# Start of the high weight blocks in 512-column tiles, and the order of products in the k-outer routine

## The chip, the core and the metric

The kernel runs on one core of one Trainium2 chip. The metric is the device time of one execution in microseconds. Before the change it is 2354.62 us, the median of 3 runs (2353.46 to 2354.73).

## The reference

Two layers of an encoder over 16 meta tokens and 256 tokens (272 rows, width 2048). Each layer projects the stream once (`w_in`, 6176 columns), runs gated linear attention on one part and 2-D neighbourhood attention on another, projects both back (`w_out`), adds and normalises, and does a squared-ReLU MLP of width 8192 with a second add and normalisation. All in float32; the meta rows are dropped at the end.

```python
def _layer(h, ...):
    proj = jnp.einsum('bld,dp->blp', h, w_in)
    ...
    y_gla = _gla_mixer(gq, gk, gv, gr, glr, gla_w_up, gla_b_up, gla_norm_w)
    y_na = _na_mixer(nq, nk, nv, na_rel_bias).astype(h.dtype)
    mix = jnp.einsum('blm,md->bld', jnp.concatenate([y_gla, y_na], axis=-1), w_out)
    h = _layer_norm(DEEPNORM_ALPHA * h + mix, ln1_w, ln1_b)
    ff = jnp.einsum('blf,fd->bld', jnp.square(jax.nn.relu(jnp.einsum('bld,df->blf', h, w_ff1))), w_ff2)
    return _layer_norm(DEEPNORM_ALPHA * h + ff, ln2_w, ln2_b)
```

Nearly all of the arithmetic is the four weight products `w_in`, `w_out`, `w_ff1` and `w_ff2`.

## The kernel before

**High and low parts.** Activations are held transposed, features on the 128 partitions and tokens along a row. Each float32 operand of a weight product is split in two fp32r parts: the high part is the value cast to fp32r (ScalarE), the low part is the value less the high part (VectorE). A product of a weight block w and an activation chunk x is the sum of three matmuls: high w by high x, high w by low x, low w by high x.

**Tiles of weights.** The host lays the weights out in tiles of 128 x 1024 words (512 KB): eight blocks of 128 x 128. `order` lists them in the order of use, `made` (line 180) takes one: a DMA from SP into `raw`, then in `halves` (line 208) a cast by ScalarE into `wh` (line 211) and a subtraction by VectorE into `wl` (line 212). `weights` keeps two tiles ahead, and each of `raw`, `wh` and `wl` has three buffers.

**Where blocks stand in a tile.** `blocks` (line 194) takes the start of the first block, the step from an even block to the odd one behind it, and the step from pair to pair, in words; `block` (line 199) gives the block j that a matmul loads, and `pairs` the same blocks for the engines that write them. A high tile is dense: first 0, step 128, pair 256 words, so that every high block starts at a multiple of 256 bytes. A low tile is 1280 words wide (`WIDE`) with gaps after `LOWS` (line 42), which has two entries, picked by the tile's flag `once`:

- `once` False: starts at 0 and 576 bytes, and every 1280 bytes from there. Modulo 256 the low blocks start at 0, 64, 0, 64, ...
- `once` True: first at 32 bytes, then every 640. Modulo 256 they start at 32, 160, 32, 160, ...

**Two kinds of tiles.** `once` is set for products over exactly the 256 tokens, almost all in layer 2, where the meta rows aren't needed any more. There the high and the low half of an activation are streamed by one matmul of 512 columns ("512-column tiles"), and the low weights by a second one of 256 columns. `TURNS` (line 43) alternates them, h w h w, sixteen matmuls a tile. The other tiles have three matmuls for each block, mostly of 272 columns (272 + 2 or 256 + 2 where a norm is folded in), in the order h l h l w w, twenty-four a tile: h is high by high, l high weights by low activations, w low weights by high activations.

**Two routines.** `by_m` (line 276) goes output by output: for each output m it takes tiles of eight k chunks (`eight`, line 232, matmuls at line 246), accumulating in one PSUM bank. `by_k` (line 257, matmuls at line 272) is used where activations become ready one after the other: it holds four outputs (eight in the form `wide`) in as many banks and goes through k two chunks at a time; a tile has the blocks of two chunks j and four outputs m, block 4j + m. It is called six times: at the start of layer 1 (`wide`, 16 tiles, while x is still being loaded and split), at the start of layer 2, after the attention of each layer (`w_out`), and in the MLP of each layer: the latter five take 8 tiles each. In layer 2's `w_out` and MLP it has 256 columns, else 272.

The order of the 24 products of a `by_k` tile is set by the sort key of line 270. Commonly it takes all 16 products with high weights, then the 8 with low weights (within each, k chunk by k chunk, the four outputs in turn). In the last tile of a routine, and in the first unless it is `wide`, `by_output` puts the output m first: for each output four products with high weights, then two with low. The very first tile of `wide` has an order of its own, since its blocks arrive in parts (`head`, line 214).

TensorE takes its instructions in program order. SP issues the DMAs of the weights in the order of `order`.

Of the kernel before, what the change touches and what calls it, by code (L numbers as in the profile page):

```python
# [8 lines left out]
F32R = mybir.dt.float32r  # L9
# [5 lines left out]
P = 128  # L15
# [11 lines left out]
WB = 1024  # L27
# [11 lines left out]
PAD = 40  # L39
PITCH = 288  # L40
WIDE = 1280
LOWS = {True: (8, P + 32, 2 * P + 64), False: (0, P + 16, 2 * P + 64)}
TURNS = {True: "hwhwhwhwhwhwhwhw", False: "hlhlwwhlhlwwhlhlwwhlhlww"}

# [12 lines left out]
class Trunk:  # L57
# [122 lines left out]
    def made(self, ap, ends, once):  # L180
        if ap is None:
            return None
        nc = self.nc
        raw = self.wp.tile([P, WB], F32, name="raw", tag="raw")
        wh, wl = self.wp.tile([P, WB], F32R, name="wh", tag="wh"), self.wp.tile([P, WIDE], F32R, name="wl", tag="wl")
        wh, wl = self.blocks(wh, 0, P, 2 * P), self.blocks(wl, *LOWS[once])
        for c in map(slice, (0,) + ends, ends):
            nc.sync.dma_start(raw[:, c], ap[:, c])
            self.halves(raw[:, c], wh, wl, slice(c.start // P, c.stop // P))
        if not ends:  # L190
            self.head(ap, raw, wh, wl)
        return wh, wl
# [64 lines left out]
    def by_k(self, acts, n, before, wide=False):  # L257

        ps = [self.pm.tile([P, 512], F32, name="mm", tag="mm") for _ in range(4)]
        if wide:  # L260
            ps += [self.bank() for _ in range(4)]
        nk = len(acts)
        for k in range(0, nk, 2):
            before(k)
            for g in range(0, len(ps), 4):
                wh, wl = self.weights()
                parts = ((wh, 0), (wh, 1), (wl, 0))
                order = [(j, p, m) for j in range(2) for p in range(3) for m in range(4)]
                by_output = k == nk - 2 or k == 0 and not wide
                order.sort(key=lambda o: (o[0], o[2] // 2) if wide and not k + g else (by_output and o[2], o[1] // 2))  # L270
                for j, p, m in order:
                    self.nc.tensor.matmul(ps[g + m][:, :n], lhsT=self.block(parts[p][0], 4 * j + m), rhs=acts[k + j][parts[p][1]][:, :n],  # L272
                                          start=k + j + p == 0, stop=k == nk - 2 and j + p == 3)
        return [p[:, :n] for p in ps]

# [836 lines left out]
def layout(inputs):  # L1112
    import numpy as np

    a = {k: np.asarray(v) for k, v in inputs.items()}
    f = np.float32
    x = np.concatenate([a["x"][0], a["meta"]], axis=0)
    o = {"xT": x.reshape(L, DC, P).transpose(2, 1, 0)}
    w = a["w_in"]
    q, k, v, r = w[:, :, 0:512], w[:, :, 512:1024], w[:, :, 1024:2048], w[:, :, 2048:3072]  # L1120
    lr, nq, nk, nv = w[:, :, 3072:3104], w[:, :, 3104:4128], w[:, :, 4128:5152], w[:, :, 5152:6176]
    c = lambda m, j: m[:, :, j * P:j * P + P]
    cols = [k, v[:, :, :512], q, v[:, :, 512:], r] + [c(m, j) for j in range(8) for m in (nq, nk, nv)]

    def tiles(m, kinds, halves=1):

        d, kk, n = m.shape
        nk = kk // P // halves
        m = m.reshape(d, halves, nk, P, n // 512, 512).transpose(0, 1, 4, 2, 3, 5)
        out = np.empty((d, halves, n // 512, nk // 2, P, WB), f)  # L1130
        for g in range(n // 512):
            s = m[:, :, g]
            for l in range(d):
                if (l, g) in kinds:
                    t = s[l].reshape(halves, nk // 2, 2, P, 512).transpose(0, 1, 3, 2, 4)
                else:
                    t = s[l].reshape(halves, nk // 8, 8, P, 4, P).transpose(0, 4, 1, 3, 2, 5)
                out[l, :, g] = t.reshape(halves, nk // 2, P, WB)
        return out if halves > 1 else out[:, 0]

    o["win"] = tiles(np.concatenate(cols, axis=2), ((0, 0), (0, 1), (1, 1)))
    w, q = o["win"][0, 0, 0], WB // 4
    o["head"] = np.stack([np.concatenate([w[:, c * q:c * q + q], o["xT"][:, c]], axis=1) for c in range(2)], axis=1)
    o["wlr"] = lr.reshape(DEPTH, DC, P, 32).transpose(0, 2, 1, 3).reshape(DEPTH, P, 512)
    o["wout"] = tiles(a["w_out"], ((0, 0), (1, 0)))
    o["wff1"] = tiles(a["w_ff1"], ((0, 2), (1, 2)))
    o["wff2"] = tiles(a["w_ff2"], (), 2)
    wup = np.zeros((DEPTH, LRK, 2, GH * GDK), f)
    for s in range(0, 96, 32):
        wup[:, s:s + 16, 0], wup[:, s + 16:s + 32, 1] = a["gla_w_up"][:, 0], a["gla_w_up"][:, 1]  # L1150
    wup[:, 96] = wup[:, 97] = a["gla_b_up"]
    o["wup"] = wup
    low = np.zeros(LRK, bool)
    low[64:96] = low[97] = True
    o["sel"] = np.stack([low, 1 - 2 * low], axis=1).astype(f)
    per = lambda m: m.reshape(DEPTH, DC, P).transpose(0, 2, 1)
    o["vec"] = np.concatenate([per(a["ln1_w"]), per(a["ln1_b"]), per(a["ln2_w"]), per(a["ln2_b"]),
                               a["gla_norm_w"].reshape(DEPTH, 2, P).transpose(0, 2, 1)], axis=2)
    o["norm"] = np.stack([a["ln2_w"][-1], a["ln2_b"][-1]])
    p = np.arange(P)  # L1160
    rb = a["na_rel_bias"]
    nab = np.zeros((DEPTH, NAH, 2, P, NKEY), f)
    qr, qc = p // 32, p % 32
    for t in range(2):
        kr = np.concatenate([p // 32, np.arange(32) // 8])
        kc = np.concatenate([t * 32 + p % 32, (32, 24)[t] + np.arange(32) % 8])
        cc = t * 32 + qc
        cs = np.clip(cc - WIN_W // 2, 0, GW - WIN_W)
        inside = (kc[None] >= cs[:, None]) & (kc[None] < cs[:, None] + WIN_W)
        dr = kr[None] - qr[:, None] + WIN_H - 1  # L1170
        dc = np.clip(kc[None] - cc[:, None], -(WIN_W - 1), WIN_W - 1) + WIN_W - 1
        nab[:, :, t, :, :160] = np.where(inside, rb[:, :, dr, dc], f(NEG))
    o["nab"] = nab.reshape(DEPTH, 8, 4, P, NKEY).transpose(0, 1, 3, 2, 4)
    xor = p[:, None] % 32 ^ p[None, :32]
    lev = np.where(xor == 0, 0, np.floor(np.log2(np.maximum(xor, 1))) + 1)
    o["mask"] = np.stack([lev == i + 1 for i in range(5)], axis=1).astype(f)
    o["ident"] = np.eye(P, dtype=f)
    qm = np.zeros((NM, NK2), f)
    qm[:, :32] = NEG
    o["qmask"] = qm  # L1180
    return {k: np.ascontiguousarray(v) for k, v in o.items()}
# [24 lines left out]
```

## Time and profile before

| what | value |
|---|---|
| median of 3 runs | 2354.62 us |
| the profiled execution's own time | 2354.79 us |
| its span, from first to last instruction | 2353.0 us |
| granted TensorE clock, mean | 0.999 |
| matmuls | 18180 |
| weight tiles loaded (512 KB each) | 766, beside the parts of the first two |
| HBM read | 414.03 MB |

The page's first part gives the busy time of each engine: PE is the matmuls of TensorE, PEld its weight loads, DVE is VectorE, ACT ScalarE. [...] The fourth part follows the work that ended last back to the start. In the timeline a row is a group of equal instructions in sequence: start in us, time to the end of the last, engine, line, operation, what it writes and reads, shape, count, and in brackets how long the engine had been idle and what ended it. In a window's row stand the time and the busy time and count of PE and PEld, the granted clock, and the DMA's share and rate.

### The profile page before, as it was taken

Reading aid. Unit: us, or ns where it says so; the run is one execution under the profiler, and the core shown is the slowest. Engines: PE = TensorE matmul, PEld = TensorE weight load, DVE = VectorE, ACT = ScalarE, POOL = GpSimd, SP = SyncE. Lnnn points to the kernel's source line nnn. Section 1 sums busy time; section 2 is a strip of 40 time slices with the busy share of each in tenths; the row PEclk is TensorE's granted clock in tenths of the full one; section 3 lists DMA queues with packets and bytes.
Section 4 is the critical chain, followed back from the end, with each engine's and each line's share of the span. In section 5 each row is a group of like instructions: output and inputs, shape, how many; then the busy total and the mean of one; then the engine's idle time right before and its main releaser. Section 6 shows DMA issues by size and latency. Waiting matters only on the chain.

```text
span 2353.0 us, 44603 instructions
## 1 busy us (share of the span) xinstructions
PE 2342.2 (100%) x18180; PEld 2222.5 (94%) x18180; DVE 1528.2 (65%) x2432; ACT 1213.0 (52%) x2100; POOL 130.2 (6%) x200
## 2 busy tenths in 40 slices
PE   9999999999999999999999999999999999999998
PEld 9999999999999999999999899999988888888888
DVE  5588777775544455557576887778766555666655
ACT  5666664564433344444456666655644333444443
POOL 0021110100000000000020121101000000000000
PEclk9999999999999999999999999999999999999999
DMA  8454445555555555555555454555566656566564
GB/s 256 153 164 155 152 141 179 170 178 181 180 180 179 180 180 180 181 180 178 179 190 165 154 173 154 162 170 186 184 191 190 187 188 187 188 189 213 191 190 147
DMA packets 118301, 419.02 MB, mean 178 GB/s; under 512 B 13512, under 2 KB 14024, under 8 KB 118096
## 3 DMA queue, kind: packets, MB, share of 16 engines
q1 hardware_dynamic: 117808, 415.65, 55.9%
q8 instruction: 142, 2.33, 0.4%
q10 hardware_dynamic: 288, 0.52, 0.1%
q14 instruction: 63, 0.52, 0.1%
HBM read 414.03 MB, written 2.10 MB: 177 GB/s over the span
## 4 chain that ended last, share of the span: by engine, by line
PE 96%; DVE 1%; ACT 1%; DMA 1%; issue 0%; SPq 0%; DVEq 0%; ACTq 0%
PE mm L246 86%; PE mm L272 5%; PE bg L783 1%; DMA raw<-in_win 1%; PE mm L722 1%; PE bg L583 1%; DVE wl L212 0%; PE bg L272 0%; ACT wh L211 0%; PE bg L429 0%; DMA xraw<-in_xT 0%; PE mm L748 0%; DVE acc L1011 0%; PE bg L634 0%; PE bg L909 0%
## 5 line engine op out<-in xcount | busy, mean ns | idle before, releaser
L212 DVE TENSOR_TENSOR wl<-raw,wh 128x1024 fp32r<-128x1024 f32 (+1 forms) x770 | 941.8, 1224 | 657.1 <-ACT wh L211 648.7
L211 ACT CAST wh<-raw 128x1024 fp32r<-128x1024 f32 (+1 forms) x770 | 805.1, 1046 | 905.9 <-PE mm L246 669.8
L246 PE MATMUL mm<-x,wh 128*128 128x272 f32 (+3 forms) x5376 | 1099.3, 309 | 0.1
L246 PEld LDWEIGHTS mm<-x,wh 128*128 128x128 f32 x5376 | 803.6, 188 | 51.6 <-PE mm L722 0.6
L246 PE MATMUL mm<-x,wl 128*128 128x272 f32 (+3 forms) x3264 | 753.4, 283 | 0.3 <-DVE wl L212 0.2
L246 PEld LDWEIGHTS mm<-x,wl 128*128 128x128 f32 x3264 | 548.3, 188 | 0.6 <-DVE wl L212 0.6
L246 PE MATMUL mm<-y,wh 128*128 128x272 f32 (+2 forms) x2128 | 477.3, 320 | 0.0
L246 PEld LDWEIGHTS mm<-y,wh 128*128 128x128 f32 x2128 | 328.9, 188 | 29.9
L246 PE MATMUL mm<-u,wh 128*128 128x272 f32 (+2 forms) x1552 | 347.0, 320 | 0.0
L246 PE MATMUL mm<-y,wl 128*128 128x272 f32 (+1 forms) x1408 | 338.8, 282 | 0.0
L246 PEld LDWEIGHTS mm<-u,wh 128*128 128x128 f32 x1552 | 239.4, 188 | 21.5
L246 PE MATMUL mm<-u,wl 128*128 128x272 f32 (+1 forms) x1024 | 246.1, 282 | 0.0
L246 PEld LDWEIGHTS mm<-y,wl 128*128 128x128 f32 x1408 | 242.2, 188 | 0.0
L246 PEld LDWEIGHTS mm<-u,wl 128*128 128x128 f32 x1024 | 176.2, 188 | 0.0
L272 PE MATMUL mm<-x,wh 128*128 128x272 f32 (+1 forms) x512 | 73.4, 288 | 1.0 <-DVE x L295 0.5
L272 PEld LDWEIGHTS mm<-x,wh 128*128 128x128 f32 x512 | 67.5, 189 | 1.5 <-DVE x L295 0.7
L999 POOL TENSOR_SCALAR acc<-acc,vec 128x272 f32<-128x272 f32 (+1 forms) x24 | 41.9, 1751 | 273.6 <-DVE acc L1011 155.0
L560 ACT COPY U<-S 128x272 f32<-128x272 f32 (+1 forms) x104 | 40.4, 429 | 20.6 <-DVE S L569 19.7
L871 DVE TENSOR_TENSOR acc<-acc,mm 128x256 f32<-128x256 f32 (+1 forms) x71 | 30.2, 425 | 31.3 <-PE mm L246 30.7
L569 DVE TENSOR_TENSOR S<-S,dec 128x272 f32<-128x272 f32 (+1 forms) x112 | 46.6, 445 | 3.7 <-ACT U L560 2.7
L294 ACT CAST u<-ft 128x272 fp32r<-128x272 f32 (+1 forms) x64 | 26.3, 410 | 41.8 <-DVE ft L827 41.7
L571 POOL TENSOR_TENSOR dec<-dec 128x272 f32<-128x272 f32 (+6 forms) x56 | 30.2, 539 | 239.8 <-DVE S L569 239.8
(265 smaller groups left out, 1631.5 us busy)
## 6 DMA issues: line engine op xcount, KB each, us to landing
raw<-in_wff SPq DMA_DIRECT2D x512, 512.0 KB, 3.7
raw<-in_win SPq DMA_DIRECT2D x190, 512.0 KB, 3.9
raw<-in_wout SPq DMA_DIRECT2D x64, 512.0 KB, 3.6
nb<-in_nab SPq DMA_DIRECT2D x16, 352.0 KB, 4.1
xraw<-in_xT SPq DMA_DIRECT2D x7, 272.0 KB, 5.9
out<-out SPq DMA_DIRECT2D x5, 256.0 KB, 3.1
brow<-in_norm SPq DMA_DIRECT2D x4, 256.0 KB
gw<-in_wup SPq DMA_DIRECT2D x4, 196.0 KB
```

Of the source, the lines that this page charges most:

```text
L211: self.nc.scalar.copy(h, r)
L212: self.wl = self.nc.vector.tensor_tensor(lo, r, h.bitcast(F32), ALU.subtract).ins
L246: mm(o, lhsT=self.block(w, j), rhs=rhs, start=first and not i, stop=last and i == len(TURNS[once]) - 1)
L272: self.nc.tensor.matmul(ps[g + m][:, :n], lhsT=self.block(parts[p][0], 4 * j + m), rhs=acts[k + j][parts[p][1]][:, :n], start=k + j + p == ...
L294: self.nc.scalar.copy(hi, src)
L560: nc.scalar.copy(U[:, lv % 4, j, :w].rearrange("p (n t h) -> p n t h", t=2, h=hb), bass.AP(S.tensor, S.offset + 2 * j * L, [S.ap[0], [2 * ...
L569: tt(o, o, totals(lv, odd, w), ALU.mult)
L571: nc.gpsimd.tensor_tensor(d[1], d[1], d[0], ALU.mult)
L583: nc.tensor.matmul(ps[b * 32:b * 32 + 32, o:o + w], lhsT=k[:, c:c + 32], rhs=q[:, r:r + w], start=True, stop=True)
L722: nc.tensor.matmul(ps[hh][:, t * NKEY:t * NKEY + NKEY], lhsT=q[hs, NM + t * P:NM + t * P + P], rhs=k[hs, t, :], start=True, stop=True)
L871: tt(a, a, part, ALU.add)
L999: nc.gpsimd.tensor_scalar(a, a, gain, bias, ALU.mult, ALU.add)
```

## The change

The high tile gets the width of the low one, 1280 words, and its first block a start picked by `once` (`HIGHS`): 24 words (96 bytes) in 512-column tiles, 0 as before in the others. Step and pair stay 128 and 256 words, so in 512-column tiles every high block starts 96 bytes past a multiple of 256.

In `by_k` every tile is now taken output by output, save those of the first two k chunks in the form `wide`. So that its low blocks stand as in `by_m`, block 2m + j is now that of output m and chunk j, except in those first tiles, and `layout` on the host stores the tiles so (the first tile of each of the two `wide` groups is put back into the old order).

```diff
+HIGHS = {True: 24, False: 0}
...
-        wh, wl = self.wp.tile([P, WB], F32R, name="wh", tag="wh"), self.wp.tile([P, WIDE], F32R, name="wl", tag="wl")
-        wh, wl = self.blocks(wh, 0, P, 2 * P), self.blocks(wl, *LOWS[once])
+        wh, wl = (self.wp.tile([P, WIDE], F32R, name=nm, tag=nm) for nm in ("wh", "wl"))
+        wh, wl = self.blocks(wh, HIGHS[once], P, 2 * P), self.blocks(wl, *LOWS[once])
...
-                by_output = k == nk - 2 or k == 0 and not wide
-                order.sort(key=lambda o: (o[0], o[2] // 2) if wide and not k + g else (by_output and o[2], o[1] // 2))
+                first = wide and not k
+                order.sort(key=lambda o: (o[0], o[2] // 2) if first and not g else (not first and o[2], o[1] // 2))
                 for j, p, m in order:
-                    self.nc.tensor.matmul(ps[g + m][:, :n], lhsT=self.block(parts[p][0], 4 * j + m), rhs=acts[k + j][parts[p][1]][:, :n],
+                    self.nc.tensor.matmul(ps[g + m][:, :n], lhsT=self.block(parts[p][0], 4 * j + m if first else 2 * m + j), rhs=acts[k + j][parts[p][1]][:, :n],
...
-                    t = s[l].reshape(halves, nk // 2, 2, P, 512).transpose(0, 1, 3, 2, 4)
+                    t = s[l].reshape(halves, nk // 2, 2, P, 4, P).transpose(0, 1, 3, 4, 2, 5)
...
     w, q = o["win"][0, 0, 0], WB // 4
+    for t in o["win"][0, :2, 0]:
+        t[:] = t.reshape(P, 4, 2, P).transpose(0, 2, 1, 3).reshape(P, WB)
```

## The prediction

> **What bounds the kernel now.** I read the page first: busy time, granted clock and chain.
>
> ```profile
> PE 2342.2 (100%) x18180; PEld 2222.5 (94%) x18180; DVE 1528.2 (65%) x2432; ACT 1213.0 (52%) x2100; POOL 130.2 (6%) x200
> PEclk9999999999999999999999999999999999999999
> PE 96%; DVE 1%; ACT 1%; DMA 1%; issue 0%; SPq 0%; DVEq 0%; ACTq 0%
> L246 PE MATMUL mm<-x,wh 128*128 128x272 f32 (+3 forms) x5376 | 1099.3, 309 | 0.1
> ACT wh L211 <- PE mm L272: 38.0, 20, 2.7
> ```
>
> TensorE fills the span, the clock is never held back, 96% of the chain that ended last is TensorE, and the largest group waited 0.1 us in all. The last row, from the list of waits, is the reverse direction: ScalarE waits for TensorE to release a high buffer. So time can only come from the pace of the products (the step from one matmul's start to the next one's), and be lost where the new order makes TensorE wait. A matmul's own duration (309 ns) is longer than its step and tells nothing about pace; I take steps from starts.
>
> The second view is a window wholly inside the 512-column tiles, with the groups by shape that count them; then the timeline of TensorE at five places.
>
> ```profile
> 1700.00:1800.00 100.00, 100.00 (x573) 87.58 (x573) 1.00 0.61 188
> L246 PE MATMUL mm<-x,wh 128*128 128x512 f32 x1152 | 405.3, 395 | 0.0
> L246 PE MATMUL mm<-y,wh 128*128 128x512 f32 x688 | 242.3, 394 | 0.0
> L246 PE MATMUL mm<-u,wh 128*128 128x512 f32 x496 | 175.0, 394 | 0.0
> ```
>
> 573 products in 100 us are 175 ns each, or 350 ns for a pair of one 512-column high and one 256-column low product. There are 1152 + 688 + 496 = 2336 such pairs: some 817 us, a third of the span.
>
> ```profile
> 1240.11 2.19 PE L272 MATMUL mm<-x,wh 128*128 128x272 f32 x16
> 1242.13 1.16 PE L272 MATMUL mm<-x,wl 128*128 128x272 f32 x8
> 1243.13 0.67 PE L272 MATMUL mm<-x,wh 128*128 128x272 f32 x4
> ...
> 1246.13 0.40 PE L246 MATMUL mm<-x,wh 128*128 128x512 f32 x1
> ```
>
> This is the k-outer routine at 272 columns. A tile in the old order (16 high products, then 8 low) takes 1243.13 - 1240.11 = 3.02 us; the last tile, which is already taken output by output, 3.00. The same 24 products in the m-outer routine:
>
> ```profile
> 433.16 0.65 PE L246 MATMUL mm<-y,wh 128*128 128x272 f32 x4
> ...
> 433.90 0.65 PE L246 MATMUL mm<-y,wh 128*128 128x272 f32 x4
> ...
> 434.63 0.41 PE L246 MATMUL mm<-y,wh 128*128 128x272 f32 x2
> ```
>
> Twelve products take 1.47 us, so a tile takes 2.94. At 256 columns (k-outer; then the one slim group of the m-outer routine):
>
> ```profile
> 1546.43 2.08 PE L272 MATMUL mm<-y,wh 128*128 128x256 f32 x16
> 1548.35 1.11 PE L272 MATMUL mm<-y,wl 128*128 128x256 f32 x8
> 1549.30 0.28 PE L272 MATMUL mm<-y,wh 128*128 128x256 f32 x1
> ...
> 2328.50 0.63 PE L246 MATMUL mm<-y,wh 128*128 128x256 f32 x4
> ...
> 2331.34 0.28 PE L246 MATMUL mm<-y,wh 128*128 128x256 f32 x1
> ```
>
> In the first tile the sixteen highs, all of whose blocks start at a multiple of 256 bytes, step by (1548.35 - 1546.43) / 16 = 120.0 ns; the eight lows, whose blocks start alternately 0 and 64 bytes past one, by 0.95 / 8 = 118.75. Shape, clock and activations are the same; what differs is where the weights start. The slim group, whose low starts are mixed as well, takes 2.84 us for its 24 products against 2.87: again 1.25 ns each. So the start of a weight block seems to be worth about a nanosecond of pace, in a kernel that is nothing but pace. That is the lever of this change.
>
> **The change, part by part.** The built programs hold the same instructions on every engine: products, casts, subtractions and DMAs. POOL keeps its order, SP swaps two pairs of issues, ScalarE moves 36 instructions and VectorE 93 by a few places, none of them around the wait priced below. The high tile grows from 1024 to 1280 words, and what is allocated behind it moves by whole multiples of 256 bytes. These cost nothing: ScalarE and VectorE are at 52% and 65%, and TensorE, the cover, is busy all the time; should a cast come late, 1 us of it would be 1 us of the span.
>
> *k-outer order.* Six middle tiles of each routine go from 3.02 to 2.94 us, its first and last from 3.00 to 2.94, since order and low starts (0, then 64, for the two k) become those of the m-outer routine: 6 x 0.08 + 2 x 0.06 = 0.60 us. Three routines run 272 columns without the wide form: -1.8. Two run 256 columns, 2.865 to 2.84 over 8 tiles each: -0.4. The wide one has 14 changed tiles (the first pair keeps its order), some -1.0.
>
> Against it, each tile now needs its low weights after 4 products, not 16, some 1.5 us sooner, and the second activation after 2 instead of 8. Behind the waiting product everything on TensorE queues. Where are lows late? In the layer-2 routine:
>
> ```profile
> 1225.02 2.17 PE L272 MATMUL mm<-x,wh 128*128 128x272 f32 x16
> 1225.07 1.43 DVE L212 TENSOR_TENSOR wl<-raw,wh 128x1024 fp32r<-128x1024 f32 x1
> 1227.03 1.17 PE L272 MATMUL mm<-x,wl 128*128 128x272 f32 x8
> ```
>
> VectorE ends these lows at 1226.50. Sixteen highs covered that (first low at 1227.03); four cover until 1225.02 + 0.49 = 1225.51. TensorE then stands for 1.0 us: +1.0. Next tile's lows (VectorE again, 1.2 us on) are then in time. In the wide routine:
>
> ```profile
> 32.15 1.22 DVE L212 TENSOR_TENSOR wl<-raw,wh 128x1024 fp32r<-128x1024 f32 x1 [2.65 <-ACT wh L211]
> 32.53 2.19 PE L272 MATMUL bg<-x,wh 128*128 128x272 f32 x16
> ...
> 36.37 0.79 DVE L295 TENSOR_TENSOR x<-xraw,x 128x272 fp32r<-128x272 f32 x2
> ...
> 36.87 0.39 PE L272 MATMUL mm<-x,wh 128*128 128x272 f32 x1 [0.53 <-DVE x L295]
> ...
> 39.48 2.19 PE L272 MATMUL bg<-x,wh 128*128 128x272 f32 x16
> ```
>
> By the tile of 32.53 TensorE would be some 0.4 us early, but the lows end at 33.37, so its last 20 products end at 33.4 + 2.45 = 35.9 instead of 35.6. The next tile needs the second low activation (36.37 + 0.79 = 37.16) in its fourth product: 37.2 + 21 x 0.1225 = 39.8 instead of 39.48. Five more tiles at 0.06 to 0.08 win the 0.3 back: 0 net. The later release of the high buffer (after product 22 instead of 16) falls on the 38.0 us that ScalarE waits anyway, with casts two tiles ahead. k-outer in sum: -1.8 - 0.4 + 1.0 + 0 = -1.2 us; bounds -3.2 (no wait is new) and +0.8 (the waits stay, the pace gains only at half).
>
> *High blocks 96 bytes on.* In a 512-column tile the low blocks start alternately 32 and 160 past a multiple of 256, and the highs move from 0 to 96: each load then starts 64 bytes (modulo 256) from the load before it, the spacing of the 118.75 ns lows. No row shows this spacing at 512 columns, so it is bounded: gain at most the 3.3 ns per product between 3.02 and 2.94 over 24 (4672 products: -15.4 us); loss at most what an extra piece costs, from the 274-column group:
>
> ```profile
> 1218.91 0.67 PE L246 MATMUL mm<-x,wh 128*128 128x274 f32 x4
> ...
> 1219.67 0.67 PE L246 MATMUL mm<-x,wh 128*128 128x274 f32 x4
> ...
> 1220.43 0.67 PE L246 MATMUL mm<-x,wh 128*128 128x274 f32 x4
> ```
>
> Six products take 0.76 us, 126.7 ns each against 122.5 at 272. Two more columns at 272's rate (122.5 / 272) are 0.9, so 3.3 ns is something else, such as one more piece to fetch; on 2336 high loads, +7.7. Between -15.4 and +7.7 I take the row it is nearest to, the 1.25 ns of the two 256-column readings (equal activations, only starts differ), on both products of a pair, since the distance to the load before changes for both: 4672 x 1.25 ns = -5.8 us.
>
> [...]
>
> *Sum.* The profiled execution took 2354.79 us (span 2353.0 and 1.8 around it): 2354.8 - 1.2 - 5.8 = 2347.8. The median of the runs, 2354.62, is 0.2 lower: 2347.6.
>
> **Rivals** (the -1.2 stays in each unless said).
> A, the forecast: 1.25 ns on both products, 2347.6.
> B, more of it: the spacing brings the whole 3.3 ns to both products, 2354.6 - 1.2 - 15.4 = 2338.0. For it: 512-column tiles have the most weights at one start. Against: their lows are shifted already.
> C, half of it: only the 256-column product gains, since in the 512-column one a load has twice the time: 2336 x 1.25 = 2.9, 2350.5. For it: the long product's share of the 350 ns is about twice a load's step of 118.75, so a load beside it has slack.
> D, starts don't matter, and the highs' part does nothing: 2353.4. For it: the readings of 1.25 ns are at the edge of what 10 ns of timeline resolve. Against: two of them agree.
> E, slower: a 512-byte block 96 past a boundary spans one more piece than one at 0, each high load gets 3.3 ns longer, and as the low product beside it is no longer than a load, TensorE waits for it: 2354.6 - 1.2 + 7.7 = 2361.1. It decides from 0.5 ns per pair on, where it eats the -1.2. For it: the 274-column step. Against: the lows, shifted by 32 and 160, don't show it in a pair of 350. [...]
> F, new waits in the k-outer routines (second activations, reordered VectorE work) cost 3 us more than counted and highs gain little: 2356.4.
>
> **How the numbers follow.** Chances: A 0.40, B 0.16, C 0.09, D 0.13, E 0.18, F 0.04. A measurement of this kernel tells about 0.2%, 4.7 us, from no change. Faster by more than that are A and B, 0.56; C, D and half of F lie within, 0.24; E and half of F are slower, 0.20. The range 2338 to 2360 leaves out half of B and somewhat over half of E, under 0.2. A's own range, 0.6 to 2 ns per product, is 2344 to 2351.
>
> **What would show it.** A window in the 512-column tiles with more than 573 products in 100 us (577 for A, 584 for B, 573 for D, 568 for E). k-outer tiles of 2.94 us instead of 3.02, and a wait of about 1.0 us for VectorE's lows at 1225.5. The wide routine ending at the same time. I am wrong if pairs keep at 350 ns, or if line 272 shows several new waits.

## The result, and the profile after

The changed kernel takes 2341.65 us (median of 6 runs, 2340.3 to 2343.35) where the kernel before takes 2353.78 (6 runs, 2353.46 to 2354.73, the three of the time before among them). The ratio is 0.9948, with a 95% interval of 0.9935 to 0.996: 12.1 us faster. The forecast was 2347.6, with 2338 to 2360 as its range: 7.0 us below the time before of 2354.62. The direction was right; the gain is 12.1 us where 7.0 were forecast.

The page of the changed kernel, its lines for the busy engines, the granted clock, the chain that ended last, and the largest group:

```profile
PE 2328.5 (99%) x18180; PEld 2215.7 (95%) x18180; DVE 1527.6 (65%) x2432; ACT 1212.0 (52%) x2100; POOL 130.9 (6%) x200
PEclk9999999999999999999999999999999999999999
PE 96%; DVE 2%; ACT 1%; DMA 1%; issue 0%; SPq 0%; DVEq 0%; ACTq 0%
L247 PE MATMUL mm<-x,wh 128*128 128x272 f32 (+3 forms) x5376 | 1094.5, 309 | 0.1
```

The picture is the old one: as many matmuls, the clock never held back (0.999 both times), TensorE 96% of the chain. No cover has gone and no bottleneck has moved; the same products pass sooner. The profiled execution took 2342.16 us against 2354.79, span 2340.4 against 2353.0.

The same window of the 512-column tiles as in the prediction, products of `by_m` alone:

```profile
1700.00:1800.00 100.00, 100.00 (x585) 88.52 (x584) 1.00 0.63 190
```

It holds 585 products where it held 573. The forecast wanted 577, rival B 584. The timeline of TensorE inside these tiles (only the highs of four pairs are shown):

```profile
1999.93 0.39 PE L247 MATMUL mm<-x,wh 128*128 128x512 f32 x1
...
2000.27 0.39 PE L247 MATMUL mm<-x,wh 128*128 128x512 f32 x1
...
2000.62 0.39 PE L247 MATMUL mm<-x,wh 128*128 128x512 f32 x1
...
2000.96 0.39 PE L247 MATMUL mm<-x,wh 128*128 128x512 f32 x1
```

Three pairs take 1.03 us, 343 ns each where they took 350. To see in which product that lies, I took from the trace every step (one matmul's start to the next one's) in uninterrupted stretches of 512-column tiles whose activations lie without a gap (some 2010 pairs), and their means. An "even" high block is followed by a low block at the first of the two low starts, an "odd" one by the second. In ns:

```
                 512-column step     256-column step     pair
                 even      odd       even      odd       even     odd
before           231.4     233.4     117.3     117.9     348.7    351.3
after            226.8     226.8     115.1     118.3     341.9    345.1
```

The long product gained 5.6 ns (232.4 to 226.8), the short one 0.9 (117.6 to 116.7), a pair 6.5 in its mean (350.0 to 343.5): 2010 pairs make 13.1 us.

Where in the execution does the gain come? I followed the start of the same product in both profiles. The difference, this run less before, in us:

```
at (us, about)                      after    highs only   order only
end of the wide by_k          54    +0.25      -0.79        -0.82
start of by_k, layer 2      1221    -0.79      -0.65        -1.96
its end                     1246    -0.90      -0.66        -2.27
start of by_k, w_out        1527    -0.30      -0.23        -2.21
its end                     1552    -0.38      -0.23        -2.29
end of w_out's m-outer      1620    -0.41      -1.40        -1.45
start of by_k, MLP          1667    -0.40      -1.39        -1.44
its end                     1690    -0.50      -1.39        -1.55
end of 512-column tiles     2328   -12.55     -13.44        -1.55
```

(The two other columns are the first two experiments below. Executions differ by one or two us in the wide routine, those of one and the same kernel too (50.21 and 52.23 us, below), so only differences down a column count, from that routine's end on.) After 1690 us each column with the highs at 96 gains 12.05 us in one stretch, and the one with the highs at 0 gains nothing: (2328 - 1690) / 0.350 = 1823 pairs at 6.5 ns are 11.8. Ahead of that the changed kernel stands only 0.5 us better than the old one. So the 12 us are the pace of the 512-column tiles, and the new order of `by_k` is worth little by itself.

That has its parts. The k-outer tiles did become faster. The timeline of TensorE, first and last row of one tile of layer 2's routine, and then of one at 256 columns:

```profile
1239.16 0.65 PE L273 MATMUL mm<-x,wh 128*128 128x272 f32 x4
...
1242.10 0.53 PE L273 MATMUL mm<-x,wh 128*128 128x272 f32 x3
...
1546.08 0.64 PE L273 MATMUL mm<-y,wh 128*128 128x256 f32 x4
...
1548.93 0.64 PE L273 MATMUL mm<-y,wh 128*128 128x256 f32 x4
```

1242.10 - 1239.16 = 2.94 us at 272 columns (before 3.02), 2.85 at 256 (before 2.87). Taken from the start of a routine's first product to that of the first product behind it, the two routines of layer 1 went from 26.52 to 25.94 us and from 24.10 to 23.51, and to just these times in every kernel with the new order below. These are the 0.6 us each of the forecast, and they make up the step from +0.25 to -0.79 in the table. In layer 2 `w_out` and the MLP won 0.1 us each.

But TensorE waits in new places. Its list of waits (waiting product and line, releaser; us in total, times, longest), after:

```profile
PE mm L273 <- DVE x L296: 1.4, 2, 0.9
...
PE mm L247 <- DVE wl L213: 0.9, 2, 0.7
PE mm L273 <- DVE wl L213: 0.6, 1, 0.6
```

and before:

```profile
PE mm L272 <- DVE wl L212: 0.6, 1, 0.6
PE mm L272 <- DVE x L295: 0.5, 1, 0.5
...
PE mm L246 <- DVE wl L212: 0.2, 1, 0.2
```

The first row is the wide routine. The second product of a tile now needs the low part of the first activation, where in the old order the fifth did. Its timeline (VectorE makes the low parts of both activations in the row ahead):

```profile
17.20 0.79 DVE L296 TENSOR_TENSOR x<-xraw,x 128x272 fp32r<-128x272 f32 x2
...
17.69 0.75 PE L273 MATMUL mm<-x,wh 128*128 128x272 f32 x3 [0.47 <-DVE x L296]
...
36.55 0.79 DVE L296 TENSOR_TENSOR x<-xraw,x 128x272 fp32r<-128x272 f32 x2
...
37.05 0.74 PE L273 MATMUL mm<-x,wh 128*128 128x272 f32 x3 [0.91 <-DVE x L296]
```

Waits of 0.47 and 0.91 us, where before there was one of 0.53. Reckoned as in the column above, this execution stands at -0.37 at 10 us and at +0.25 at the routine's end, 0.6 us lost. The product that waits the second time starts at 37.05, when the first of the two low parts is done (36.99); by the trace the fourth, which needs the second low part, comes 0.36 us behind it. So it is the first low part that TensorE stands for, not the second as the prediction had it. But 0.6 us is no price of the new order. The routine takes 50.21 us here and 52.23 in another execution of the same kernel (the last experiment), 47.9 to 50.6 in the nine other kernels with the new order, and 48.6 to 49.95 in the three with the old one. In this stretch ScalarE waits for the DMAs of the weights and of x, five times by 1.5 to 3.7 us before and four times by 2.4 to 3.1 us after (waits over 1.5 us), here for example:

```profile
34.33 1.05 ACT L212 CAST wh<-raw 128x1024 fp32r<-128x1024 f32 x1 [3.11 <-DMA raw<-in_win]
```

These waits differ from one execution to the next, and what the new order is worth in the wide routine is not shown.

The wait for the lows of line 247 is a place that the prediction did not look at, the norm of layer 2, in 512-column tiles and outside `by_k`. After (timeline; VectorE's lows, the accumulation just ahead of them, and the product that waits):

```profile
1558.88 1.23 DVE L213 TENSOR_TENSOR wl<-raw,wh 128x1024 fp32r<-128x1024 f32 x1 [1.51 <-ACT wh L212]
...
1565.76 0.42 DVE L938 TENSOR_TENSOR s<-s,sqv 128x256 f32<-128x256 f32 x1
...
1566.10 1.22 DVE L213 TENSOR_TENSOR wl<-raw,wh 128x1024 fp32r<-128x1024 f32 x1
...
1567.37 0.39 PE L247 MATMUL mm<-y,wl 128*128 128x256 f32 x1 [0.66 <-DVE wl L213]
```

and VectorE's lows in the same stretch before:

```profile
1561.34 1.22 DVE L212 TENSOR_TENSOR wl<-raw,wh 128x1024 fp32r<-128x1024 f32 x1
...
1564.32 1.22 DVE L212 TENSOR_TENSOR wl<-raw,wh 128x1024 fp32r<-128x1024 f32 x1
```

Before, VectorE took a tile's lows about every 3 us. After, its program has the norm's accumulations between two of them, 7.2 us apart (1558.88 to 1566.10), and TensorE runs dry. From 1552 to 1620 us the pace should bring some 1.2 us, and highs alone do (-0.23 to -1.40); the changed kernel gets 0.03, so about 1.1 us are lost, and order alone loses 0.84 at the same place.

One more small loss: from 1246 to 1527 us some 300 pairs stream activations whose two halves lie apart (the second starts 128 bytes past a multiple of 256). These take 354 ns in the mean after and 352 before: +0.6 us in the column.

### The profile page after: what moved, and what is told of

It is laid out like the page before. It is cut to its first block, busy times and chain, and to the rows that moved or that the text cites. A ratio compares the mean times of both kernels' runs of the same rounds, so it can differ in the third digit from the quotient of the medians.

```text
span 2340.4 us, 44604 instructions
## 1 busy us (share of the span) xinstructions
PE 2328.5 (99%) x18180; PEld 2215.7 (95%) x18180; DVE 1527.6 (65%) x2432; ACT 1212.0 (52%) x2100; POOL 130.9 (6%) x200
## 4 chain that ended last, share of the span: by engine, by line
PE 96%; DVE 2%; ACT 1%; DMA 1%; issue 0%; SPq 0%; DVEq 0%; ACTq 0%
PE mm L247 85%; PE mm L273 6%; PE bg L784 1%; PE bg L273 1%; PE mm L723 1%; DVE wl L213 1%; PE bg L584 1%; PE bg L430 0%; ACT wh L212 0%; DMA xraw<-in_xT 0%; PE mm L749 0%; DVE acc L1012 0%; DMA raw<-in_win 0%; PE bg L635 0%; PE bg L910 0%
## 5 line engine op out<-in xcount | busy, mean ns | idle before, releaser
L273 PE MATMUL mm<-x,wh 128*128 128x272 f32 (+1 forms) x512 | 84.4, 287 | 1.5 <-DVE x L296 1.4
L273 PE MATMUL mm<-x,wl 128*128 128x272 f32 (+1 forms) x256 | 51.9, 285 | 0.6 <-DVE wl L213 0.6
## 6 DMA issues: line engine op xcount, KB each, us to landing
nb<-in_nab SPq DMA_DIRECT2D x16, 352.0 KB, 4.0
```

## The experiments

In all of them the highs' starts and the lows' two starts are meant in 512-column tiles and modulo 256 bytes, written "0; 32, 160" for before and "96; 32, 160" for the changed kernel.

**The two parts alone.** First the kernel before with the highs at 96 only (the old order in `by_k`), then the changed kernel with the highs back at 0.

```diff
+HIGHS = {True: 24, False: 0}
-        wh, wl = self.wp.tile([P, WB], F32R, name="wh", tag="wh"), ...
-        wh, wl = self.blocks(wh, 0, P, 2 * P), self.blocks(wl, *LOWS[once])
+        wh, wl = (self.wp.tile([P, WIDE], F32R, name=nm, tag=nm) for nm in ("wh", "wl"))
+        wh, wl = self.blocks(wh, HIGHS[once], P, 2 * P), self.blocks(wl, *LOWS[once])
```

> The kernel before with the high start of 96 bytes alone, k-outer routine in the old order. Theory S (the pace follows the distance, modulo 256, of each weight load's start from the start of the load before it): pairs of a 512- and a 256-column product go from 350 to about 344.7 ns as in the changed kernel, the whole is about 11 us below before, and k-outer tiles stay at 3.02 us. Theory N (most of the gain is the new product order): not more than 3 us below before.

```diff
-HIGHS = {True: 24, False: 0}
+HIGHS = {True: 0, False: 0}
```

> The changed kernel with the high start put back to 0. Theory S: pairs at 350 ns, k-outer tiles at 2.93 us, the whole 0.5 to 1.5 us below before. Theory N: 9 us or more below before.

Highs alone: 2341.27 us (2340.5 to 2341.93) against 2354.36, ratio 0.9944 (0.9931 to 0.9956). Order alone: 2353.45 (2352.21 to 2354.63), ratio 0.9996 (0.9987 to 1.0005). Windows of 200 us in the last stretch, first highs alone (columns: time; busy time and count of PE, PEld, DVE, ACT and POOL; clock, DMA share, GB/s):

```profile
1700.00:1900.00 200.00, 200.00 (x1167) 177.06 (x1166) 118.14 (x149) 87.06 (x112) 0.00 (x0) 1.00 0.65 192
```

Then order alone, and below it the kernel before:

```profile
1700.00:1900.00 200.00, 200.00 (x1145) 174.52 (x1144) 115.40 (x146) 85.88 (x110) 0.00 (x0) 1.00 0.63 189
```

```profile
1700.00:1900.00 200.00, 200.00 (x1144) 175.17 (x1144) 115.86 (x146) 86.26 (x111) 0.00 (x0) 1.00 0.60 188
```

Between these kernels the gain is the highs' start, all of it. The order's worth is 0.9 us with an interval that takes in no change. The list of waits of highs alone shows that the wait in the norm belongs to the order. With highs alone line 247 waits for lows as little as in the kernel before:

```profile
PE mm L247 <- DVE wl L213: 0.2, 1, 0.2
```

while order alone has

```profile
PE mm L273 <- DVE x L296: 0.9, 1, 0.9
...
PE mm L247 <- DVE wl L213: 0.8, 2, 0.5
```

**Is it the spacing of loads?** The prediction's reason, theory S, was that a load is quick when it starts 64 bytes (modulo 256) from the load before. Two kernels make that spacing in another way: the lows moved to 64, 192 with the highs at 0, and the highs at 224 with the old lows (224 is 64 from 32 and from 160). The rivals say that a place counts, not a distance between loads: that of the weights against the activations being streamed (X), or that of the weights by itself (Y).

```diff
-HIGHS = {True: 24, False: 0}
-LOWS = {True: (8, P + 32, 2 * P + 64), ...
+HIGHS = {True: 0, False: 0}
+LOWS = {True: (16, P + 32, 2 * P + 64), ...
```

> The changed kernel with the high blocks of 512-column tiles back at 0 and the low ones at 64 and 192 instead of 32 and 160: the same distances between loads as in the changed kernel, everything 96 bytes earlier against the activations. Theory S: pairs at 344 to 346 ns, as changed. Theory X (what counts is where a load starts against the activations streamed beside it, which start at multiples of 256): pairs clearly elsewhere, since every load's start against them differs.

```diff
-HIGHS = {True: 24, False: 0}
+HIGHS = {True: 56, False: 0}
```

> The changed kernel with high starts at 224 bytes. The distances to the lows at 32 and 160 are 64 either way, modulo 256, as with 96. Theory S: pairs at 344 to 346 ns. Theory X: elsewhere, 348 ns or more being as likely as not.

2354.01 us (2352.54 to 2356.1), ratio 0.9999 (0.999 to 1.0008), and 2354.05 (2353.4 to 2356.03), ratio 1.0 (0.9991 to 1.0009). The same window, lows moved:

```profile
1700.00:1900.00 200.00, 200.00 (x1145) 174.68 (x1144) 115.42 (x146) 86.56 (x110) 0.00 (x0) 1.00 0.63 188
```

Highs at 224:

```profile
1700.00:1900.00 200.00, 200.00 (x1145) 174.47 (x1144) 115.42 (x146) 86.32 (x110) 0.00 (x0) 1.00 0.63 188
```

Both have the spacing and not the gain: S falls.

**A place against the activations, or by itself?** The next kernel keeps the highs at 0 and moves everything else, so that all three starts stand to each other as in the changed kernel: lows at 64, 192 and the gapless activations 160 bytes on (96, 32, 160 and 0, all 160 bytes further, are 0, 192, 64 and 160; the two lows change places). The other one moves only the activations in the changed kernel.

```diff
+SHIFT = 40
-HIGHS = {True: 24, False: 0}
-LOWS = {True: (8, P + 32, 2 * P + 64), ...
+HIGHS = {True: 0, False: 0}
+LOWS = {True: (16, P + 32, 2 * P + 64), ...
...
         flat = both.rearrange("p a c -> p (a c)")
+        flat = flat[:, SHIFT:] if dense else flat
```

> Run e3 (highs at 0, lows at 64 and 192) with the dense activations of layer 2 started 160 bytes on, so that weights and activations stand to each other as in the changed kernel, all 96 bytes earlier modulo 256. Theory X (place of weights against activations): dense pairs at 343 to 344 ns as in the changed kernel. Theory Y (the absolute place of the weight blocks alone counts): 350 ns as in e3.

```diff
+SHIFT = 40
...
         flat = both.rearrange("p a c -> p (a c)")
+        flat = flat[:, SHIFT:] if dense else flat
```

> The changed kernel with the dense activations of layer 2 started 160 bytes on, weights untouched. Theory X: dense pairs leave 343.5 ns, most likely to 347 or more. Theory Y: they stay at 343.5.

All moved: 2340.11 us (2339.39 to 2343.58) against 2353.88, ratio 0.9945 (0.993 to 0.996). Activations moved: 2360.41 (2359.19 to 2363.04), ratio 1.0028 (1.0018 to 1.0039). The window, all moved:

```profile
1700.00:1900.00 200.00, 200.00 (x1167) 177.09 (x1166) 117.34 (x149) 87.37 (x110) 0.00 (x0) 1.00 0.65 193
```

Activations moved, window and then timeline of TensorE:

```profile
1700.00:1900.00 200.00, 200.00 (x1133) 173.48 (x1133) 114.90 (x145) 85.01 (x109) 0.00 (x0) 1.00 0.64 187
```

```profile
1999.82 0.40 PE L249 MATMUL mm<-x,wh 128*128 128x512 f32 x1
...
2000.17 0.40 PE L249 MATMUL mm<-x,wh 128*128 128x512 f32 x1
...
2000.88 0.40 PE L249 MATMUL mm<-x,wh 128*128 128x512 f32 x1
```

With nothing but the activations 160 bytes on, three pairs take 1.06 us, 353 ns each, slower than before the change; with the weights 160 bytes on as well they take 343.5, and the even and odd steps of the changed kernel come back exchanged, as the lows are. X holds and Y falls: how weights and activations stand to one another counts, and the place of the weights by itself does not give the pace (with highs at 0 and lows at 64, 192 a pair takes 350.2 ns with the activations in one place and 343.5 in the other).

**Which start is best?** The changed kernel with another start of the highs, and once with both lows at 32 (dense).

```diff
-LOWS = {True: (8, P + 32, 2 * P + 64), ...
+LOWS = {True: (8, P, 2 * P), ...
```

> The changed kernel with all low blocks of 512-column tiles dense from 32 bytes, so that each starts at 32 modulo 256 instead of 32 and 160 in turn. If the low block's own start makes the 256-column product 115.1 or 118.3 ns, all become 115.1, pairs 341.8, and the whole is about 3.5 us below the changed kernel. If it is the place of the next high block (even or odd), the alternation stays and so does the time.

```diff
-HIGHS = {True: 24, False: 0}
+HIGHS = {True: 16, False: 0}
```

> The changed kernel with high starts at 64 bytes. Theory X has no number for it before it is seen: one more point of the pace against the start. If a start of 96 is a narrow optimum, pairs are at 347 ns or more; if it is a broad one, below 346.

```diff
-HIGHS = {True: 24, False: 0}
+HIGHS = {True: 20, False: 0}
```

> The changed kernel with high starts at 80 bytes, between 64 (pairs of 353.2 and 340.3 ns in turn) and 96 (341.9 and 345.1). If the pace goes over smoothly from one start to the next, the mean of a pair is about 345 to 346 ns and the time between that of 64 and that of 96; if the two good halves meet, it is below 342 and the time below the changed kernel's.

```diff
-HIGHS = {True: 24, False: 0}
+HIGHS = {True: 28, False: 0}
```

> The changed kernel with high starts at 112 bytes, on the other side of 96. A broad optimum has the mean of a pair at 343 to 346 ns; a narrow one at 348 or more.

The window for lows dense, and below it for highs at 64, at 80 and at 112:

```profile
1700.00:1900.00 200.00, 200.00 (x1138) 174.10 (x1137) 115.48 (x146) 86.05 (x110) 0.00 (x0) 1.00 0.62 187
```

```profile
1700.00:1900.00 200.00, 200.00 (x1155) 175.07 (x1155) 116.75 (x149) 86.73 (x111) 0.00 (x0) 1.00 0.64 190
```

```profile
1700.00:1900.00 200.00, 200.00 (x1134) 172.79 (x1133) 114.92 (x145) 85.06 (x109) 0.00 (x0) 1.00 0.62 187
```

```profile
1700.00:1900.00 200.00, 200.00 (x1137) 173.91 (x1136) 114.50 (x144) 85.20 (x109) 0.00 (x0) 1.00 0.61 187
```

All kernels together, with the mean steps worked out from the starts as above, the pair's mean, and the time (ratio to the kernel before with its interval). "acts" is the start of the gapless activations against that of the kernel before.

```
highs; lows; acts          512-col step    pair    time us   ratio
                           even    odd     mean
0; 32,160; 0   (before)    231.4   233.4   350.0   2353.78
0; 32,160; 0   (new order) 231.7   233.7   350.0   2353.45   0.9996 (0.9987 to 1.0005)
0; 64,192; 0               229.7   235.9   350.2   2354.01   0.9999 (0.999 to 1.0008)
224; 32,160; 0             235.0   231.4   350.0   2354.05   1.0    (0.9991 to 1.0009)
96; 32,160; 0  (after)     226.8   226.8   343.5   2341.65   0.9948 (0.9935 to 0.996)
0; 64,192; 160             226.8   226.8   343.5   2340.11   0.9945 (0.993 to 0.996)
96; 32,160; 160            238.9   232.5   353.2   2360.41   1.0028 (1.0018 to 1.0039)
96; 32,32; 0               234.1   234.1   351.9   2357.63   1.0016 (1.0008 to 1.0025)
64; 32,160; 0              235.0   227.0   346.8   2347.79   0.9977 (0.9966 to 0.9989)
80; 32,160; 0              235.3   235.3   352.7   2359.57   1.0024 (1.0014 to 1.0033)
112; 32,160; 0             232-237 *       352.5   2358.59   1.0018 (1.0009 to 1.0027)
* from block to block of a tile
```

The time follows the pair: 2010 pairs by the difference to 350.0 ns give -13.1, -6.4, +3.8, +5.0, +5.4 and +6.4 us for 343.5, 346.8, 351.9, 352.5, 352.7 and 353.2, and the runs lie at -12.1 (or -13.8), -6.1, +3.7, +4.1, +5.1 and +6.5 from their kernel before. 96 is a narrow place: 16 bytes to either side lose the whole gain and more. At 80 neither of the two outcomes came that I expected (345 to 346 ns or below 342), and 64, at 346.8, lies between what I had called a narrow and a broad place.

Starts modulo 256 do not say everything either. In the kernel before, blocks 1 and 3 of a tile have the same starts modulo 256, and so have their neighbours, but from 1690 to 2328 us their high products step by 234.4 and 232.3 ns in the mean. With the highs at 112 the eight blocks of a tile step by 232 to 237 ns with no even and odd pattern.

Dense lows were a miss. I expected both lows at 32 to bring every pair to the better value of the even ones (341.9); they brought 351.9. The same high (96), the same low (32) behind it and the same activations take 226.8 ns when the low loaded ahead of that high was at 160, and 234.1 when it was at 32. Modulo 256 nothing but the odd low blocks' starts differs between the two, and the nearest of these to an even high block is the one loaded ahead of it. Block 0, whose own starts are the same in full, shows it as well: 226.7 and 234.2 ns from 1690 to 2328 us. So what went before matters too, and no rule for one load or one pair of starts describes this.

**Neither the highs nor the order.** The next kernel is the one before with the moved lows and activations, highs at 0 and the old order. The changed kernel ran again beside it.

```diff
+SHIFT = 40
-LOWS = {True: (8, P + 32, 2 * P + 64), ...
+LOWS = {True: (16, P + 32, 2 * P + 64), ...
...
         flat = both.rearrange("p a c -> p (a c)")
+        flat = flat[:, SHIFT:] if dense else flat
```

> The kernel before, k-outer routine in its old order, with highs left at 0, lows at 64 and 192 and the dense activations of layer 2 started 160 bytes on (the relative places of e5). Theory X: dense pairs at 343.5 ns, about 13 to 15 us below before, the same as or 1 us below the changed kernel: that would show that nothing of the gain needs the highs to move, or the new order.

> The changed kernel once more, on the same chip as e11: 11 to 13 us below before, so that the two can be set side by side.

2340.22 us (5 runs, 2339.5 to 2340.42), ratio 0.9941 (0.9927 to 0.9954), beside 2341.98 (5 runs, 2340.6 to 2344.16), ratio 0.995 (0.9937 to 0.9962). The window of the former:

```profile
1700.00:1900.00 200.00, 200.00 (x1167) 177.03 (x1167) 117.28 (x148) 87.35 (x110) 0.00 (x0) 1.00 0.66 193
```

Its pace is that of the changed kernel. The gain needs neither moved highs nor the new order. All five of its runs lie below all five of the changed kernel's, some 1.8 us by the medians, though the intervals of the ratios overlap. Some of that has a place: its 300 pairs with separate halves take 351 ns in the mean and not 354, about 1 us, and the wait in the norm belongs to the new order. The new order in turn wins 1.2 us in layer 1. That the old order is better is not shown: the same starts with the new order took 2340.11 us, and these two are the fastest kernels of these runs.

## Why the prediction was right, and where its steps failed

**Direction and bound: right.** "In a kernel that is nothing but pace" held: every us gained or lost by the starts is in steps of TensorE, with clock, counts, ScalarE and VectorE the same (before and after: 0.999 and 0.999, 18180 products, ScalarE 1213.0 and 1212.0 us busy, VectorE 1528.2 and 1527.6).

**The highs' term: right in sign, less than half its size, and for a reason that fell.** "1.25 ns on both products of a pair, 4672 x 1.25 = -5.8 us": measured are 5.6 ns on the long product and 0.9 on the short one, 6.5 a pair instead of 2.5. Its two readings (118.75 ns against 120.0, and 2.84 us against 2.87) were taken as the worth of a spacing of 64 bytes between loads. Two other kernels with this spacing gained nothing, and a third, the changed kernel with its activations moved, lost 3.2 ns a pair. So the row that the term was taken from does not price this edit, although it pointed at starts. That this edit gained at all was luck as far as its reason goes: of the four sets of places with this spacing that ran, one gains, two change nothing and one loses, and highs at 80 or 112 lost. The bounds, -15.4 and +7.7, hold for all kernels of the table: 6.5 ns a pair is next to the lower one (6.6), and the worst starts cost 6.5 us.

**The count of pairs was a little high.** 2336 were counted by shape; some 300 of them have activations in two separate halves, and these lost 2 ns instead of gaining. A count by shape puts them together.

**The k-outer term: its tiles right, its waits wrong.** Tiles went to 2.94 us as forecast and to 2.85 at 256 columns (forecast 2.84), and layer 1's two routines won 0.6 us each as forecast. "TensorE then stands for 1.0 us" in the layer-2 routine was off. Its second tile (timeline):

```profile
1224.20 1.64 PE L273 MATMUL mm<-x,wh 128*128 128x272 f32 x12
...
1224.29 1.43 DVE L213 TENSOR_TENSOR wl<-raw,wh 128x1024 fp32r<-128x1024 f32 x1
...
1225.77 1.03 PE L273 MATMUL mm<-x,wl 128*128 128x272 f32 x6
...
1226.64 0.67 PE L273 MATMUL mm<-x,wh 128*128 128x272 f32 x4
```

The built program does not take this tile output by output: twelve highs, of three outputs, stand ahead of six lows. They cover VectorE until 1224.20 + 12 x 0.1225 = 1225.67, and the lows end at 1225.72: the first low is 0.1 us late, the six take 0.87 us instead of 0.74, and some 0.2 us are lost, not 1.0. The prediction took the order of this tile from the source's sort key, and the built program has another. The routine went from 24.94 to 24.82 us, and in the other kernels with the new order it takes 24.6 to 25.2; the forecast was 0.4 more than before. On the other side the norm of layer 2 took 1.1 us. That is rival F's mechanism, VectorE work reordered, with a third of its price: the prediction's "none of them around the wait priced below" says nothing of waits that were not priced. Its 0 for the wide routine had the wrong activation behind the wait, as told above, and is in size neither borne out nor refuted, since that routine differs by more from one execution to the next. Forecast -1.2 for the whole term; by the runs between +0.4 (the changed kernel against highs alone, 2341.65 and 2341.27) and -0.9 (order alone), with no change inside the interval.

**The rivals.** A is too small. B has the size of the pair, 6.6 ns, but not its mechanism: not 3.3 on both products, and not from the spacing. C is the wrong way round: the long product gained most (5.6 ns against 0.9), so its length did not shield it. D falls: with nothing changed but the start of the activations a pair goes from 343.5 to 353.2 ns. E, one more piece from a start off a boundary, falls by the gain, and by highs at 224, which take 350.0 as at 0. But a start can cost nearly what E said (7.7 us): at 80 and 112 the kernel is 4 to 5 us slower than before.

**Left open.** Why these starts and not others. Weights against activations matter (343.5 or 353.2 ns a pair), what was loaded ahead of a high block matters (a step of 226.8 or 234.1 ns), and 16 bytes decide (343.5 ns a pair at 96, 352.7 at 80), but no model that I formed gives the table, and no run here shows what in the hardware makes a start quick or slow. One pattern may help: from 1690 to 2328 us the mean pair is 350.0 ns in four kernels whose even and odd high products step by quite different times (before, the new order, 224, and 0; 64,192), and 343.3, 346.7 or 353.3 in others, as if the mean went in steps of 3.3 ns. Highs at 80 and at 112 and dense lows (352.7, 352.5 and 352.0) do not fit it. The new order's worth stays open as well.

## What to carry to other kernels

Where TensorE alone sets the time, the starts of weight blocks and activations in a partition are a knob: here they gained up to 0.6% or cost up to 0.3%. It has no safe default and no rule yet: move one start in 16- or 32-byte steps, count products in a window inside the stretch concerned, and look at the whole set (high and low weights, activations, order of loads), since the highs' start that is best with one set (96, 343.5 ns a pair) is among the worst with another (353.2). And when an order is edited, read the built program's own order, on VectorE also and outside the edited routine, since it can differ from the source's.

## What of the hardware was not expected

- The step of a 512-column fp32r product ran from 226.8 to 238.9 ns with the starts of weights and activations alone, at a granted clock of 0.999 to 1.0. The 256-column one behind an odd high took 118.3 ns in the changed kernel and 113.3 with highs at 64 (a pair of 340.3 less a step of 227.0).
- Moving only the high weights from 80 to 96 to 112 bytes gave pairs of 352.7, 343.5 and 352.5 ns.
- Moving all operands together (160 bytes, modulo 256) changed nothing (343.5 ns a pair both times); moving the activations alone cost 9.7 ns a pair (353.2).
- An even high product's step was 226.8 ns with the odd low blocks at 160, the one loaded ahead of it among them, and 234.1 with them at 32; its own start, the low block behind it and the activations were the same.
